# Differential attention with TensorE's order written out piece by piece

## The chip, the cores and the metric

One core of one Trainium2 chip. The metric is the device time of one execution in microseconds (us). Times inside the execution are microseconds from the start of the profiled span.

## The reference

A trunk of four layers over 256 tokens of width 1024, in float32. Each layer is a feed-forward half step, a token mixer and a second feed-forward half step, with a norm before and after each. The mixers of the four layers are sparse attention (layer 0), stick-breaking attention (layer 1), differential attention (layer 2) and sparse attention again (layer 3). Only the third is touched by the change:

```python
qa, ka, va = jnp.split(h @ w_in, 3, axis=-1)
q = qa.reshape(B, T, DIFF_HEADS, 2, DIFF_DH)      # 8 heads, 2 maps each, 64 wide
k = ka.reshape(B, T, DIFF_HEADS, 2, DIFF_DH)
v = va.reshape(B, T, DIFF_HEADS, 2 * DIFF_DH)
...
    s = jnp.einsum('bqhmd,bkhmd->bhmqk', qb, k).astype(f32) * scale
    s = jnp.where(dist >= 0, s - slopes[None, :, None, None, None] * dist, NEG)
    p = jax.nn.softmax(s, axis=-1)
    a = p[:, :, 0] - lam_full * p[:, :, 1]
    o = jnp.einsum('bhqk,bkhe->bqhe', a.astype(v.dtype), v)
    o = rms_norm(o, subln_g) * (1.0 - lam_init)
...
return sweep_blocks(block, T) @ w_out
```

So each head makes two softmax maps, subtracts one from the other, multiplies by the values and norms the result; an output projection follows.

## The kernel before

The whole trunk is one program. Activations stay on the chip; the weights stream through it once. A weight piece of 512 KB is loaded into one of seven raw buffers by the queue of SyncE (SP), then split into a high part (a cast on ScalarE, line 135) and a low part (a subtraction on VectorE, line 136). High and low parts have nine buffers each (`NSPLIT`). Every projection is three products per row block: high by high, and the two mixed ones. For the sums the activations too are held as a high and a low part, `yh` and `yl`.

PSUM has eight banks in three pools: four named `acc` (projections, value products, output sums), two `mm` (scores) and two `tp` (transposes).

The tokens stand in two halves of 128, `h` = 0 and 1; causality lets half 0 see 128 keys and half 1 see 256. In the differential mixer the eight heads stand in two groups of four. The four combinations of group and half are named a (group 0, half 0), b (group 0, half 1), c (group 1, half 0) and d (group 1, half 1), and each is worked in two units of two heads. One unit has these steps: scores (line 663, into both `mm` banks), the softmax of `softmax_alibi` (VectorE reads the banks, adds the distances and takes the maximum at line 666; ScalarE exponentiates at line 674; ScalarE and VectorE scale and subtract at lines 1137 and 1138), transposes of the result (line 1145), their copy to SBUF, and the value products (line 1150). When a combination's two units are through, its four heads are normed (lines 1158 to 1165), transposed (line 1170) and written to `yh` and `yl` (`put_o`, lines 627 and 628) for the output projection (lines 405 to 409).

A scheduler turns the program's text into an order for each engine. The text is the first guess, and an instruction may move ahead of another on its engine where nothing forbids it. `tc.issue_after(ins)` forbids it: what is traced under it stays behind `ins` on the engine of `ins`. The helper `pin` (line 304) uses this to chain pieces of TensorE's work, so that each piece's matmuls stay behind the last matmul of the piece before; matmuls for the conditioning weights (`ada`) are left out of the chain. The sparse mixers (`Nsa`) already run a `plan` of pinned pieces and a `rest` of pinned output projections behind it. The differential mixer, like the stick-breaking one, is not pinned: its `plan` lists whole projections (192 matmuls of 256 columns for queries or keys of a part, less where pairs are named) and lets generators a to d advance by stages between them.

The mixer's end goes over into the next sublayer. `post` for half 0 (residual and norm of the output sums) and `pre` for half 0 (the next sublayer's norm, the transposes `p_y` of line 339, and the modulation) are traced between the mixer's body and its `tail`; the tail holds the output projections of half 1 that are left. `pre` is pinned only where the mixer is sparse:

```python
post(i, s, 0, cur.accs[0], last)
...
(pin if s == 1 and not i % 3 else lambda f: f())(lambda: gate.extend(pre(*subs[n + 1], 0)))
cur.tail()
```

Of the kernel before, what the change touches and what calls it, by code (L numbers as in the profile page):

```python
# [40 lines left out]
def trunk_kernel(ctx, tc, x, c, ada_w, ada_b, norm_g, ffn_w1, ffn_w2, nsa_w_in, nsa_cmp_pe, nsa_cmp_w1,  # L41
# [650 lines left out]
    class Nsa(Mixer):  # L692
# [11 lines left out]

        def run(self, plan):


            for op in plan.replace("\n", " ").split(";"):
                op, *args = op.split()
                if args and args[0] in "abcd":  # L710
                    pin(getattr(self.at[args[0]], op), *map(int, args[1:]))
                else:
                    pin(getattr(self, op), *map(int, args))

        def body(self):
            pinned[:] = []
            self.at = {c: self.Attend(self, *half) for c, half in zip("abcd", HALVES)}
            self.run(self.plan)

        def tail(self):  # L720
            self.run(self.rest)
# [157 lines left out]

        def weight(self, k):  # L880
            gate_on[:] = self.copied
            self.wo[k] = self.out_weight(k)
            gate_on[:] = []

        def o(self, h, k, n=None):

            ns = (0, 1) if n is None else (n,)
            accs = self.accs.setdefault(h, [None, None])
            for m in ns:
                if accs[m] is None:  # L890
                    accs[m] = bank("acc", [128, 512], f"o{h}{m}")
            tok = slice(h * 128, (h + 1) * 128)
            mm_acc(accs, yh[:, k, tok], yl[:, k, tok], self.wo[k], k == 0, k == KC - 1, ns)
# [201 lines left out]
    class Diff(Dense):  # L1095
        w_in, w_out = diff_w_in, diff_w_out
        q_scale = staticmethod(lambda j: 0.125 / dslopes[j])
        plan = [("proj", 1, 0,), ("proj", 0, 0,), 'a', ("proj", 1, 1,), 'b', 'a', ("proj", 0, 1,), 'c', 'b', 'ab', 'c', 'd', ("out_proj", 0, 0,), 'c', 'd', ("out_proj", 1, 0,), 'd']
# [24 lines left out]
        def attend(self, hg, h, _):  # L1123
            tok = slice(h * 128, (h + 1) * 128)
            po = bank("acc", [128, 4, 128], "p_o")

            def heads(hp):
# [41 lines left out]
            for j in range(4):  # L1169
                nc.tensor.transpose(p[:, j, :], o[:, j, :], ident)  # L1170
# [118 lines left out]
```

## Time and profile before

| | |
|---|---|
| median of 3 runs | 2169.16 us (2161.97 to 2175.18) |
| the profiled execution's own time | 2169.74 us |
| its span | 2167.9 us |
| TensorE busy in the span | 2096.4 us (97%) |
| VectorE, ScalarE busy | 1622.9 us (75%), 1119.8 us (52%) |
| mean granted clock of TensorE | 0.99 |
| differential mixer, from the last value projection to the next sublayer's first product | 1321.2 to 1420.4 us |

The span is the stretch from the first to the last instruction that the profile records. "Granted clock" is the share of the full clock that TensorE was given: 1.00 is 2.4 GHz, 0.50 is 1.2 GHz. The ends of matmuls are modelled, so neighbouring matmuls overlap in the rows; the distance between their starts is the pace.

### The profile page before, as it was taken

Reading aid. Unit: us, or ns where it says so; the run is one execution under the profiler, and the core shown is the slowest. Engines: PE = TensorE matmul, PEld = TensorE weight load, DVE = VectorE, ACT = ScalarE, POOL = GpSimd, SP = SyncE. Lnnn points to the kernel's source line nnn. Section 1 sums busy time; section 2 is a strip of 40 time slices with the busy share of each in tenths; the row PEclk is TensorE's granted clock in tenths of the full one; section 3 lists DMA queues with packets and bytes.
Section 4 is the critical chain, followed back from the end, with each engine's and each line's share of the span. In section 5 each row is a group of like instructions: output and inputs, shape, how many; then the busy total and the mean of one; then the engine's idle time right before and its main releaser. Section 6 shows DMA issues by size and latency. Waiting matters only on the chain.

```text
span 2167.9 us, 37376 instructions
## 1 busy us (share of the span) xinstructions
PE 2096.4 (97%) x14395; PEld 1856.1 (86%) x14395; DVE 1622.9 (75%) x2736; ACT 1119.8 (52%) x1989; POOL 67.3 (3%) x154
## 2 busy tenths in 40 slices
PE   5999999999999999999999999999999999999998
PEld 5999775899899979799989888789999997668998
DVE  7987866777798777677688858687779868767654
ACT  3444655644544456754464455664455445656443
POOL 1000000000000000100000000000000000000000
PEclk9999998999999999999999999999999999999999
DMA  9998752687699856388779958278869986545761
GB/s 316 335 348 287 252 137 78 215 287 262 199 330 312 282 186 222 122 278 277 256 235 330 313 170 297 78 240 274 275 203 330 308 276 194 163 118 172 241 200 59
DMA packets 338179, 512.55 MB, mean 236 GB/s; under 512 B 20832, under 2 KB 211256, under 8 KB 338000
## 3 DMA queue, kind: packets, MB, share of 16 engines
q1 hardware_dynamic: 329456, 501.15, 69.9%
q10 hardware_dynamic: 8544, 9.01, 1.4%
q8 instruction: 113, 1.85, 0.3%
q14 instruction: 66, 0.54, 0.1%
HBM read 507.91 MB, written 1.05 MB: 235 GB/s over the span
## 4 chain that ended last, share of the span: by engine, by line
PE 74%; DVE 11%; issue 5%; DMA 5%; ACT 4%; POOL 2%; ACTq 0%; SPq 0%; DVEq 0%; POOLq 0%
PE p_gu L386 12%; PE p_gu L388 12%; PE p_gu L387 12%; PE f L405 6%; PE f L406 6%; PE f L409 6%; DVE lo_w L136 3%; DMA raw_ada<-in_ada_w_dram 3%; PE p_o L909 1%; PE p_pr L386 1%; PE p_pr L387 1%; PE p_pr L388 1%; PE p_t L956 1%; POOL rx L325 1%; PE o L405 1%
## 5 line engine op out<-in xcount | busy, mean ns | idle before, releaser
L135 ACT CAST hi_w<-raw_w 128x1024 fp32r<-128x1024 f32 x528 | 551.5, 1055 | 325.6 <-PE f L409 113.4
L136 DVE TENSOR_TENSOR lo_w<-raw_w,hi_w 128x1024 fp32r<-128x1024 f32 x528 | 633.1, 1221 | 103.6 <-ACT hi_w L135 97.2
L386 PE MATMUL p_gu<-yh,hi_w 128*128 128x256 f32 x2368 | 665.6, 281 | 4.0 <-DVE yh L351 4.0
L387 PE MATMUL p_gu<-yl,hi_w 128*128 128x256 f32 x2368 | 660.9, 279 | 0.3 <-DVE yl L352 0.3
L388 PE MATMUL p_gu<-yh,lo_w 128*128 128x256 f32 x2368 | 661.0, 279 | 0.0
L386 PEld LDWEIGHTS p_gu<-yh,hi_w 128*128 128x128 f32 x2368 | 445.7, 188 | 17.3 <-DVE lo_w L136 6.2
L192 DVE SCALAR_TENSOR_TENSOR ada_acc<-raw_ada,cT,ada_acc 128x512 f32<-128x512 f32 x500 | 374.0, 749 | 103.3 <-DMA raw_ada<-in_ada_w_dram 95.3
L387 PEld LDWEIGHTS p_gu<-yl,hi_w 128*128 128x128 f32 x2368 | 446.0, 188 | 5.4 <-issue 1.7
L388 PEld LDWEIGHTS p_gu<-yh,lo_w 128*128 128x128 f32 x2368 | 445.8, 188 | 0.2
L405 PE MATMUL f<-hi_w,hb 128*128 128x512 f32 x704 | 275.8, 393 | 1.9 <-ACT hb L550 1.8
L406 PE MATMUL f<-lo_w,hb 128*128 128x512 f32 x704 | 275.9, 392 | 0.0
L409 PE MATMUL f<-hi_w,hb 128*128 128x512 f32 x704 | 228.3, 391 | 0.0
L550 ACT CAST hb<-sg 128x256 fp32r<-128x256 f32 x148 | 60.2, 407 | 199.6 <-DVE sg L549 198.1
L548 ACT ACTIVATE sg<-p_gu 128x256 f32<-128x256 f32 x148 | 56.3, 380 | 204.1 <-PE p_gu L388 183.8
L405 PEld LDWEIGHTS f<-hi_w,hb 128*128 128x128 f32 x704 | 132.3, 188 | 29.2 <-ACT hb L550 4.7
L409 PEld LDWEIGHTS f<-hi_w,hb 128*128 128x128 f32 x704 | 131.6, 188 | 29.3 <-DVE hb L551 1.9
L406 PEld LDWEIGHTS f<-lo_w,hb 128*128 128x128 f32 x704 | 132.2, 188 | 24.5 <-DVE lo_w L136 0.3
L549 DVE TENSOR_TENSOR sg<-sg,p_gu 128x256 f32<-128x256 f32 x148 | 61.5, 416 | 79.0 <-ACT sg L548 78.8
L551 DVE TENSOR_TENSOR hb<-sg,hb 128x256 fp32r<-128x256 f32 x148 | 62.4, 422 | 35.2 <-ACT hb L550 35.2
L350 ACT ACTIVATE y<-p_y,ab 128x128 f32<-128x128 f32 x184 | 67.2, 465 | 29.7 <-PE p_y L339 24.2
L387 PE MATMUL p_pr<-yl,hi_qk 128*128 128x256 f32 x256 | 71.8, 281 | 0.0
L386 PE MATMUL p_pr<-yh,hi_qk 128*128 128x256 f32 x256 | 71.5, 281 | 0.0
(273 smaller groups left out, 3191.6 us busy)
## 6 DMA issues: line engine op xcount, KB each, us to landing
raw_w<-in_ffn_w_dram SPq DMA_DIRECT2D x528, 512.0 KB
raw_ada<-in_ada_w_dram SPq DMA_DIRECT2D x288, 512.0 KB
raw_kv<-in_nsa_w_in_dram SPq DMA_DIRECT2D x16, 512.0 KB
raw_q<-in_nsa_w_in_dram SPq DMA_DIRECT2D x16, 512.0 KB
raw_cw<-in_nsa_cmp_w_dram SPq DMA_DIRECT2D x16, 512.0 KB
raw_wo<-in_nsa_w_out_dram SPq DMA_DIRECT2D x32, 256.0 KB
raw_qk<-in_sb_w_in_dram SPq DMA_DIRECT2D x16, 512.0 KB
raw_qk<-in_diff_w_in_dram SPq DMA_DIRECT2D x16, 512.0 KB
```

The costliest lines, as they stand in the source:

```text
L135: nc.scalar.copy(hi, src)
L136: nc.vector.tensor_sub(lo, src, hi)
L192: nc.vector.scalar_tensor_tensor(a, r[:, j], cT[:, k:k + 1], a, op0=OP.mult, op1=OP.add)
L350: nc.scalar.activation(y[:, j, :], p[:, j, :], AF.Identity, scale=ab[:, k:k + 1], bias=ab[:, 8 + k:9 + k])
L386: nc.tensor.matmul(o, cols(wh), yh[:, k, :], start=first and k == 0, stop=False)
L387: nc.tensor.matmul(o, cols(wh), yl[:, k, :], start=False, stop=False)
L388: nc.tensor.matmul(o, cols(wl), yh[:, k, :], start=False, stop=last and k == KC - 1)
L405: nc.tensor.matmul(acc[n], lh, wh[:, sl], start=first, stop=False)
L406: nc.tensor.matmul(acc[n], lh, wl[:, sl], start=False, stop=False)
L409: nc.tensor.matmul(acc[n], ll, wh[:, sl], start=False, stop=last)
L549: nc.vector.tensor_mul(sg, sg, p[:, 1, :])
L551: nc.vector.tensor_sub(hl[:, cc, :], sg, hh[:, cc, :])
```

## The change

The differential mixer becomes a pinned one. `run`, `body`, `tail`, `weight` and `o` move from `Nsa` to a new class `Pinned`, which `Nsa` and `Diff` inherit, and nothing changes in `Nsa` itself. In `Diff` the generators give way to a written plan whose pieces are:

- `pj which part j [rows]`: keys (1) or queries (0) of two heads, 48 matmuls, or with `rows` one half of the row blocks, 24 matmuls;
- `S x n`, `T x n`, `P x n`: scores with softmax, transposes with their copy (always on ScalarE), and value products of unit n of combination x; `P x 1` also norms x;
- `N x`: transposes of the normed heads and `put_o`;
- `weight k`: load and split of output weight k, issued behind the latest copy of a `T`;
- `o h k [n]`: output products of half h with weight k, six matmuls, or three for one column half n.

`pre` of half 0 is pinned behind any pinned mixer, so now behind `Diff` too, and the pieces of `rest` are pinned behind it.

```diff
+    class Pinned(Mixer):
+        def run(self, plan):
+            for op in plan.replace("\n", " ").split(";"):
+                op, *args = op.split()
+                if args and args[0] in "abcd":
+                    pin(getattr(self.at[args[0]], op), *map(int, args[1:]))
+                else:
+                    pin(getattr(self, op), *map(int, args))
+        def body(self):
+            pinned[:] = []
+            self.at = {c: self.Attend(self, *half) for c, half in zip("abcd", HALVES)}
+            self.run(self.plan)
+        def tail(self):
+            self.run(self.rest)
+        def weight(self, k):
+            gate_on[:] = self.copied
+            self.wo[k] = self.out_weight(k)
+            gate_on[:] = []
+        def o(self, h, k, n=None):
+            ns = (0, 1) if n is None else (n,)
+            accs = self.accs.setdefault(h, [None, None])
+            for m in ns:
+                if accs[m] is None:
+                    accs[m] = bank("acc", [128, 512], f"o{h}{m}")
+            tok = slice(h * 128, (h + 1) * 128)
+            mm_acc(accs, yh[:, k, tok], yl[:, k, tok], self.wo[k], k == 0, k == KC - 1, ns)
...
-    class Nsa(Mixer):
+    class Nsa(Pinned):
...
-    class Diff(Dense):
+    class Diff(Pinned, Dense):
...
-        plan = [("proj", 1, 0,), ("proj", 0, 0,), 'a', ("proj", 1, 1,), 'b', 'a', ("proj", 0, 1,), 'c', 'b', 'ab', 'c', 'd', ("out_proj", 0, 0,), 'c', 'd', ("out_proj", 1, 0,), 'd']
+        plan = """pj 1 0 0; pj 0 0 0; S a 0; pj 1 0 1 0; S b 0; pj 1 0 1 1; pj 0 0 1; S a 1; T a 0; pj 1 1 0 0; P a 0; T b 0; S b 1;
+                  pj 1 1 0 1; P b 0; T a 1; pj 0 1 0 0; P a 1; pj 0 1 0 1; S c 0; T b 1; pj 1 1 1 0; P b 1; S d 0; pj 1 1 1 1;
+                  T c 0; pj 0 1 1 0; P c 0; weight 0; pj 0 1 1 1; N a; S c 1; T d 0; weight 1; N b; S d 1; P d 0; weight 2; o 0 0;
+                  weight 3; T c 1; o 0 1; weight 4; P c 1; T d 1; weight 5; o 0 2; weight 6; P d 1; o 0 3; weight 7; N c;
+                  o 1 0 0; o 1 1 0; o 0 4; o 0 5; N d; o 0 6; o 0 7; o 1 2 0; o 1 3 0"""
+        rest = """o 1 0 1; o 1 1 1; o 1 2 1; o 1 3 1; o 1 4 0; o 1 5 0; o 1 6 0; o 1 7 0; o 1 4 1; o 1 5 1; o 1 6 1; o 1 7 1"""
...
+        def pj(self, which, part, j, rows=None):
+            o, sc = ((self.qT, self.q_scale), (self.kT, None))[which]
+            if (which, part) not in self.w:
+                self.w[which, part] = self.columns(which, part, "qk")
+            ks = range(KC) if rows is None else range(KC // 2 * rows, KC // 2 * (rows + 1))
+            if ks[0] == 0:
+                self.pp = bank("acc", [128, 2, T], "p_pr")
+            p = self.pp
+            for q in range(2):
+                for k in ks:
+                    wh, wl = self.w[which, part][k]
+                    c = chunk(2 * j + q)
+                    nc.tensor.matmul(p[:, q, :], c(wh), yh[:, k, :], start=k == 0 and q == 0, stop=False, skip_group_check=True)
+                    nc.tensor.matmul(p[:, q, :], c(wh), yl[:, k, :], start=False, stop=False, skip_group_check=True)
+                    nc.tensor.matmul(p[:, q, :], c(wl), yh[:, k, :], start=False, stop=k == KC - 1, skip_group_check=True)
+            if ks[-1] == KC - 1:
+                j0 = 4 * part + 2 * j
+                if sc is None:
+                    evac(j, o[:, j0:j0 + 2, :], p)
+                else:
+                    nc.scalar.activation(o[:, j0, :], p[:, 0, :], AF.Copy, scale=sc(j0))
+                    nc.vector.tensor_scalar(o[:, j0 + 1, :], p[:, 1, :], sc(j0 + 1), None, op0=OP.mult)
+        class Attend:
+            def S(self, hp):
...
+                r = softmax_alibi(h, qk, [sc[:, 2 * m:2 * m + 2] for m in range(2)],
...
+            def T(self, hp):
+                h, sc = self.h, self.sc[hp]
+                p = bank("tp", [128, 2, h + 1, 128], "p_t")
+                for e in range(2):
+                    for kb in range(h + 1):
+                        nc.tensor.transpose(p[:, e, kb, :], sc[:, e, kb * 128:(kb + 1) * 128], ident)
+                t = self.t[hp] = s2([128, 2, h + 1, 128], "aT")
+                self.diff.copied = [nc.scalar.copy(t, p).ins]
+            def P(self, hp):
+                h = self.h
+                if self.po is None:
+                    self.po = bank("acc", [128, 4, 128], "p_o")
+                for e in range(2):
+                    hd = 4 * self.hg + 2 * hp + e
+                    for kb in range(h + 1):
+                        nc.tensor.matmul(self.po[:, 2 * hp + e, :], self.t[hp][:, e, kb, :],
+                                         self.diff.v[:, kb, hd * 128:(hd + 1) * 128], start=kb == 0, stop=kb == h)
+                if not hp:
+                    return
...
+            def N(self):
+                p = bank("tp", [128, 4, 128], "p_ot")
+                for j in range(4):
+                    nc.tensor.transpose(p[:, j, :], self.o[:, j, :], ident)
+                put_o(p, 4 * self.hg, self.h)
...
-            (pin if s == 1 and not i % 3 else lambda f: f())(lambda: gate.extend(pre(*subs[n + 1], 0)))
+            (pin if isinstance(cur, Pinned) else lambda f: f())(lambda: gate.extend(pre(*subs[n + 1], 0)))
```

## Rows read from the trace of the kernel before

**Rows 1.** The page's busy times: us, share of the span, instructions.

```profile
PE 2096.4 (97%) x14395; PEld 1856.1 (86%) x14395; DVE 1622.9 (75%) x2736; ACT 1119.8 (52%) x1989; POOL 67.3 (3%) x154
```

**Rows 2.** Busy by stretch: length, engines, granted clock, DMA share, GB/s.

```profile
1321.20:1420.40 99.20, 93.61 (x643) 82.05 (x643) 70.88 (x187) 62.79 (x170) 5.16 (x6) 0.97 0.49 167
...
1321.20:1343.50 22.30, 22.30 (x191) 22.13 (x190) 16.86 (x20) 10.81 (x13) 0.00 (x0) 1.00 1.02 378
...
1390.90:1407.30 16.40, 15.56 (x82) 12.76 (x81) 7.51 (x26) 9.37 (x39) 2.01 (x2) 0.98 0.00 1
```

**Rows 3.** TensorE's timeline in the mixer: start, length, operation, idle before.

```profile
1343.51 0.72 PE L663 MATMUL p_s<-qkv 64*128 64x128 f32 x8
1344.15 1.98 PE L281 MATMUL p_gate<-ada_acc,ones 128*128 128x512 f32 x4
...
1346.94 0.28 PE L387 MATMUL p_pr<-yl,hi_qk 128*128 128x256 f32 x1
...
1357.91 0.28 PE L388 MATMUL p_pr<-yh,lo_qk 128*128 128x256 f32 x1
1358.12 1.13 PE L663 MATMUL p_s<-qkv 64*128 64x256 f32 x8
1359.18 0.66 PE L1145 MATMUL p_t<-ident,sc 128*128 128x128 f32 x4
...
1378.84 1.95 PE L1150 MATMUL p_o<-qkv,aT 128*128 128x128 f32 x16
1380.63 0.38 PE L1170 MATMUL p_ot<-ident,o_n 128*128 128x128 f32 x2
...
1414.14 1.06 PE L339 MATMUL p_y<-ident,xn 128*128 128x128 f32 x8 [0.41 <-DVE xn L355]
1414.96 0.48 PE L406 MATMUL o<-lo_wo,yh 128*128 128x512 f32 x1
...
1420.17 0.40 PE L409 MATMUL o<-hi_wo,yl 128*128 128x512 f32 x1
```

**Rows 4.** TensorE's waits in 1321.2 to 1420.4: us, times, longest.

```profile
PE p_s L663 <- DVE sm_m L666: 4.3, 3, 2.4
```

**Rows 5.** Busy by microsecond where the clock falls and returns.

```profile
1384.00:1385.00 1.00, 0.56 (x2) 0.53 (x3) 1.00 (x7) 0.97 (x7) 0.00 (x0) 0.90 0.82 266
...
1391.00:1392.00 1.00, 1.00 (x5) 0.83 (x4) 1.00 (x5) 0.80 (x4) 0.00 (x0) 0.68 0.00 0
...
1924.00:1925.00 1.00, 1.00 (x4) 0.19 (x2) 0.96 (x4) 0.09 (x1) 0.00 (x0) 0.56 0.05 16
...
1934.00:1935.00 1.00, 1.00 (x5) 0.81 (x4) 0.00 (x0) 1.00 (x2) 0.00 (x0) 0.82 0.00 0
```

**Rows 6.** Timelines of ScalarE and VectorE at the first query weights.

```profile
1327.72 1.05 ACT L135 CAST hi_qk<-raw_qk 128x1024 fp32r<-128x1024 f32 x1 [2.65 <-DMA raw_qk<-in_diff_w_in_dram]
...
1328.95 1.22 DVE L136 TENSOR_TENSOR lo_qk<-raw_qk,hi_qk 128x1024 fp32r<-128x1024 f32 x1
```

**Rows 7.** Timelines in layer 0's mixer, scores directly behind their projection.

```profile
260.31 0.47 ACT L775 ACTIVATE qkv<-p_pr,qscale 128x256 f32<-128x256 f32 x1
...
260.84 0.48 DVE L776 TENSOR_SCALAR qkv<-p_pr,qscale 128x256 f32<-128x256 f32 x1
...
260.84 1.36 PE L927 MATMUL p_s<-qkv 64*128 64x256 f32 x8 [1.72 <-ACT qkv L775]
```

**Rows 8.** Timelines of TensorE and VectorE, scores and softmax of c 1.

```profile
1377.60 0.70 PE L663 MATMUL p_s<-qkv 64*128 64x128 f32 x4 [0.49 <-DVE sm_m L666]
...
1384.83 0.64 DVE L1138 SCALAR_TENSOR_TENSOR sc<-sc,sm_r 128x128 f32<-128x128 f32 x2
```

**Rows 9.** TensorE's timeline, the last output products of token half 0.

```profile
1406.84 0.63 PE L409 MATMUL o<-hi_wo,yl 128*128 128x512 f32 x2
```

**Rows 10.** TensorE's timeline, two more of its idle stretches.

```profile
1361.33 1.82 PE L663 MATMUL p_s<-qkv 64*128 64x256 f32 x8 [1.49 <-DVE sm_m L666]
...
1923.29 1.58 PE L909 MATMUL p_o<-pT,vc 15*64 15x512 f32 x4 [2.52 <-DVE pT L631]
```

More of the change, by code (lines that the diff above doesn't have):

```diff
@@ L703, in trunk_kernel @@
         rest = """o 1 0 1; o 1 1 1; o 1 2 1; o 1 3 1; o 1 4 0; o 1 5 0; o 1 6 0; o 1 7 0; o 1 4 1; o 1 5 1; o 1 6 1; o 1 7 1"""
[L705 to L721, printed above, removed]
         def head(self, h, gate):
@@ L1139, in heads @@
                                                    sc[:, e, :], op0=OP.mult, op1=OP.add)
-                def second():
-                    p = bank("tp", [128, 2, h + 1, 128], "p_t")
-                    for e in range(2):
-                        for kb in range(h + 1):
-                            nc.tensor.transpose(p[:, e, kb, :], sc[:, e, kb * 128:(kb + 1) * 128], ident)
-                    t = s2([128, 2, h + 1, 128], "aT")
-                    evac(hp, t, p)
-                    for e in range(2):
-                        for kb in range(h + 1):
-                            nc.tensor.matmul(po[:, 2 * hp + e, :], t[:, e, kb, :],
-                                             self.v[:, kb, hds[e] * 128:(hds[e] + 1) * 128], start=kb == 0, stop=kb == h)
@@ L1152, in heads @@
-                return second
-            stages = self.pipeline([lambda hp=hp: heads(hp) for hp in range(2)])
-            next(stages)
-            yield
-            next(stages)
-            o = s2([128, 4, 128], "o_n")
-            ss = small([128, 4], "ssd")
-            for j in range(4):
-                nc.scalar.activation(junk[:, :128], po[:, j, :], AF.Square, accum_out=ss[:, j:j + 1])
-            nc.vector.tensor_scalar(ss, ss, 1.0 / 128, EPS, op0=OP.mult, op1=OP.add)
-            nc.gpsimd.tensor_tensor(ss, ss, mhalf, op=OP.pow)
@@ new lines, in P @@
+            def P(self, hp):
[9 more added lines that the diff above has]
+                    return
+                po = self.po
+                o = self.o = s2([128, 4, 128], "o_n")
+                ss = small([128, 4], "ssd")
+                for j in range(4):
+                    nc.scalar.activation(junk[:, :128], po[:, j, :], AF.Square, accum_out=ss[:, j:j + 1])
+                nc.vector.tensor_scalar(ss, ss, 1.0 / 128, EPS, op0=OP.mult, op1=OP.add)
+                nc.gpsimd.tensor_tensor(ss, ss, mhalf, op=OP.pow)
+                for j in range(4):
+                    nc.vector.scalar_tensor_tensor(o[:, j, :], po[:, j, :], ss[:, j:j + 1], self.diff.sg, op0=OP.mult, op1=OP.mult)
```

34 lines of the change are left out of this document (8 added, 26 removed).

## The prediction

> **What bounds the kernel now.** The page's busy shares come first: TensorE is busy for 97% of the span, VectorE for 75%, ScalarE for 52% [rows 1]. So time is gained only where TensorE idles, runs at its lower clock, or runs at less than its stream rate, and the change touches one stage: the mixer of layer 2, from the last value projection (1321.2) to the first product of the next feed-forward block (1420.4). The table by stretch gives this stage 99.2 us, 93.6 of them with TensorE busy [rows 2]. All else is taken to shift as a whole: a TensorE-bound kernel passes on what this stage loses or gains.
>
> A busy row overstates useful work, so I count the work by the spacing of matmul starts in TensorE's timeline [rows 3].
> - Query and key projections: the matmuls from 1346.94 to 1357.91 are 95, so 94 gaps of 0.1167 us. The stage has 382: 44.6 us.
> - Output projection: from 1414.96 to 1420.17 there are 22 gaps of 0.237 us. The stage has 96: 22.7 us.
> - Scores, eight instructions for each unit: of the first token half 0.64 us (1343.51 to 1344.15), of the second 1.06 (1358.12 to 1359.18), four units of each: 6.8 us.
> - Value products: 16 in 1.79 (1378.84 to 1380.63), so 48 take 5.4 us.
> - Transposes: eight in 0.82 (1414.14 to 1414.96), so 24 + 16 + 8 take 4.9 us. The gate's row sums: 2.0 us.
>
> Together 86.4 us. The stage therefore loses 99.2 - 86.4 = 12.8 us. Of that the list of waits puts 4.3 us on score matmuls that wait for VectorE to read the previous scores out of the two score banks [rows 4]. 3.4 us are clock: TensorE's granted clock is 0.50 between about 1384.8 and 1391.6 [rows 5], the level of 1.2 GHz, 6.85 us at half rate. The other 5.1 us are small waits and changes of shape between instruction streams. 12.8 us is all that the change could win, 0.6% of 2169.
>
> **The change part by part.** The instructions stay the same in number and shape; the evacuation of the transposed scores moves wholly to ScalarE, which has room. What changes is TensorE's order, which becomes fixed piece by piece. I walk through the new order and ask at each piece what it waits for.
>
> *The waits for score banks go.* Scores stand one unit at a time between half projections of 24 matmuls (24 x 0.1167 = 2.8 us), in which VectorE reads the banks. 4.3 us gone, except that two units of the last quarter (c 1 and d 1) have only eight transposes between them (0.8 us) against four reads and their start on VectorE of about 1.4: 0.6 us stays.
>
> *Query weights come earlier than they can.* Before, both halves of the first key projection (96 matmuls, 11.2 us) stand ahead of the queries. Now one half does, so the queries start at about 1326.8, and their last quarter of rows (k 6 and 7) is due at 1326.8 + 18 x 0.1167 = 1328.9. Its high part was cast only when its load landed at 1327.72, and its low part is ready at 1328.95 + 1.22 = 1330.2 [rows 6]. The DMA engines are full there (share 1.02) [rows 2], so it can't come sooner: 1.3 us lost, bounds 0 and 2.5 (a second split late).
>
> *A projection directly ahead of the scores that need it.* S a 0, S a 1 and S c 0 follow the query piece that they read; S c 1 has one set of transposes between. This occurs in the first layer's mixer, whose order is already pinned: ScalarE scales one chunk at 260.31 (0.47), VectorE the other at 260.84 (0.48), and TensorE had idled 1.72 us [rows 7], a part of it because ScalarE had come late from a cast. Without that, two such evacuations one behind the other make 1.0 us; three of these, and 0.4 for the fourth, 3.4 us, bounds 1.5 and 5.5. The wait stops the next half projection, whose weights are ready.
> The Trainium skill (PSUM — Partial Sum Buffer, section "PSUM bank collisions raise a hardware error") says that two engines must not touch one bank at once, so the two scalings of one projection bank follow each other. By it the price is 1.0 us each, with both side by side about 0.6 (one scaling and a handoff), and the sum 1.3 us less; the rows agree with the first, 260.84 being after the end of the scaling that began at 260.31.
>
> *Transposes of the last scores.* Between S c 1 and T c 1 TensorE has 0.4 + 0.4 + 1.1 + 0.9 + 1.4 = 4.2 us of its own work. Before, the same unit took from 1377.60 to 1384.83 + 0.64 = 1385.5 until its scores were ready, 7.9 us less 0.6 of scores [rows 8], while VectorE also split weights; now seven of the eight output weights are to be split in this very stretch, since they are issued behind the copies of T c 0 and later ones. With the 0.6 us of the score banks, that leaves 7.3 - 4.2 - 0.6 = 2.5 us of wait if the chain stays as slow, and none if VectorE serves it first. I take 1.7, nearer to the row, and 1.5 for T d 1, whose rows are twice as long but which has a product more ahead of it: 3.2 us, bounds 0 and 7. Queued behind them are output projections that could have run.
>
> *The next layer's transposes are pinned too.* This is the largest term. Residual, norm and scaling of token half 0 start when its last output product ends. Before, that matmul starts at 1407.07 (the second of the pair from 1406.84) [rows 9], and the transposes p_y start at 1414.14 [rows 3]: 7.1 us, of which TensorE idled only 0.4, because 25 matmuls of token half 1 and four transposes ran meanwhile. Now only o 1 2 0 and o 1 3 0, six matmuls or 1.4 us, stand between o 0 7 and the pinned p_y, and the remaining 36 output matmuls (8.5 us) are pinned behind it. With the chain at 6.7 (0.4 less, as VectorE then has no other output to split) the wait is 6.7 - 0.23 - 1.4 = 5.0 us, bounds 4.5 and 6. Nobody can fill it: all that is left on TensorE is behind it in its queue. In turn the next block's input is ready long before its first product, which no longer matters.
>
> *The clock after that wait.* TensorE's clock fell to 0.50 in this stage after the longest wait for score banks, 2.4 us [rows 4, 5], and in the last layer's mixer after an idle of 2.52, there from about 1924.1 to 1934.4 [rows 5, 10]. An idle of 1.49 us at 1361 brought no fall [rows 10]. A wait of 5.0 us is longer than any of these. I price it as the fall that goes: 6.85 us at half rate, 3.4 us; bounds 0 and 5.1 (10.3 us at half). The old fall goes, since its wait goes.
> The Trainium skill (TensorE: Matmul & The Clock Gate, section "What's actually happening") has 1.2 GHz as the state that an idle TensorE returns to and that activity lifts. By it this term is 3.4, without it 0; the trace agrees with it at both falls.
>
> *More changes of shape.* Going from a projection to scores costs 0.09 (from 1357.91 + 0.12 to 1358.12) [rows 3]; I take 0.2 us for the way there and back. The new order has some 17 rounds, the old 11: 1.2 us more. Of the old 5.1 about 1.9 are small waits counted anew above, so this remainder is 5.1 - 1.9 + 1.2 = 4.4, bounds 3 and 5.5.
>
> *The load queue.* On SP's queue the loads of the next block's weights stand behind those of the output weights, which now leave the raw buffers later, since their splits wait for the copies of T c 0, T d 0 and those after. That costs nothing: the DMA engines moved nothing from 1391 to 1407 [rows 2], and the first product comes later than before.
>
> **Sum.** New losses 0.6 + 1.3 + 3.4 + 3.2 + 5.0 + 3.4 + 4.4 = 21.3 us against 12.8: 8.5 us more. The profiled execution took 2169.74, 0.6 above the median of 2169.16, so 2178.2 for it and about 2177.6 beside the median: 0.4% slower, inside the 0.5% (10.8 us) that a measurement of this kernel can tell from no change.
>
> **The rivals.**
> - *As summed* (chance 0.5): 2177.6, own range 2172 to 2182.
> - *A second clock fall* (0.22). The waits before T c 1 and T d 1, 3.2 us within some 6, bring the clock down as the 2.4 us of before did. It decides once one of the two passes about 2.4 us. Price 3.4 and the longer wait itself, 1 to 4: 2182 to 2185, slower beyond the 0.5%. For it: VectorE's weight splits now fall there. Against: output products lie between the two.
> - *No clock fall at p_y* (0.18): by the clock's rows the unlikely side. 2177.6 - 3.4 = 2174, and with the waits before T c 1 and T d 1 halved 2172.5.
> - *The mixing wins* (0.1): weight splits stay out of the softmax chains' way, T c 1 and T d 1 don't wait, the gate's row sums fill two of the evacuation waits, and the clock holds. Place: the last quarter; it decides if the chain from S c 1 falls from 7.3 to 4.8 us, TensorE's own work there. Then 8.5 - 3.2 - 2 - 3.4 - 1.3 = -1.4 with the query weights in time: 2168. Faster than 0.5% would need 10.8 of 12.8 us back with p_y's 5.0 still lost: hardly possible, 0.03.
> - *The change does nothing of what it says* is not open: TensorE's order is in the program.
>
> **How the numbers follow.** The predicted time is that of the sum. All lower bounds together make 9.6 us of losses, 3.2 faster than before; all upper ones 32.2, 19.4 slower: 2166 to 2188.5. The range leaves out a little at the top and adds some of the runs' own spread (2161.97 to 2175.18) below: 2165 to 2187. Slower by over 0.5% (above 2180): 0.22 and a tenth of the rest, 0.29. Faster 0.03. Within: 0.68.
>
> **What would show it.** Right: an idle of 4.5 to 6 us on TensorE ahead of p_y of that mixer, with a granted clock of 0.50 behind it; no wait of scores on VectorE's reads above 1 us; p_gx some 8 us later after the last value projection. Wrong: p_y without a wait, its matmuls set among the output products; a wait before T d 1 of more than 4 us; a stage shorter than 99 us; or a changed time in the other layers.

## The result and the profile after

The changed kernel takes 2183.21 us (median of 11 runs, 2179.96 to 2191.17), the kernel before beside it 2172.32 (11 runs): ratio 1.0056, 95% interval 1.0043 to 1.0070, so 12.2 us slower (9.3 to 15.2); the two medians differ by 10.9. The forecast was 8.5 us more, 2177.6. The profiled execution took 2191.17 us, the longest of the 11. Behind the stage of the change it took 7.0 us more than the profile of before, 5.4 of them in the last layer's mixer, where the matmuls have the same order and the clock was lower. The windows view shows it from its key and value projection into the next block's first products, before and after (length, engines, granted clock, DMA share, GB/s):

```profile
1813.90:1981.50 167.60, 158.00 (x1002) 117.49 (x1001) 123.94 (x379) 99.23 (x261) 4.44 (x5) 0.97 0.54 159
1830.00:2003.00 173.00, 163.92 (x1001) 121.46 (x1000) 124.26 (x379) 99.15 (x262) 4.43 (x5) 0.93 0.52 154
```

So the whole spans are not compared here, only the stage of the change.

Page, busy times:

```profile
PE 2104.0 (96%) x14395; PEld 1859.7 (85%) x14395; DVE 1623.1 (74%) x2732; ACT 1121.1 (51%) x1993; POOL 66.0 (3%) x154
```

The work is that of [rows 1]. The stage from the last value projection to the next block's first product, by the same view, and under it the windows in which the clock falls:

```profile
1323.03:1434.90 111.87, 96.78 (x644) 83.62 (x643) 71.95 (x183) 65.03 (x175) 5.16 (x6) 0.94 0.43 145
1352.00:1354.00 2.00, 1.90 (x8) 1.06 (x9) 2.00 (x10) 0.37 (x1) 0.00 (x0) 0.81 0.90 246
1354.00:1356.00 2.00, 2.00 (x5) 0.90 (x4) 0.78 (x4) 0.89 (x5) 0.00 (x0) 0.50 0.88 313
1356.00:1358.00 2.00, 2.00 (x16) 2.00 (x16) 1.66 (x5) 1.45 (x6) 0.00 (x0) 0.84 0.29 115
1404.00:1406.00 2.00, 2.00 (x9) 1.72 (x8) 1.30 (x5) 2.00 (x3) 0.66 (x1) 0.61 0.71 234
1406.00:1408.00 2.00, 2.00 (x9) 1.81 (x9) 2.00 (x2) 0.90 (x4) 0.00 (x0) 0.54 0.06 23
1422.00:1424.00 2.00, 0.67 (x4) 0.70 (x5) 0.88 (x2) 0.00 (x0) 0.56 (x1) 0.50 0.00 0
1424.00:1426.00 2.00, 2.00 (x9) 1.81 (x9) 0.01 (x1) 1.55 (x5) 0.00 (x0) 0.50 0.00 0
1426.00:1428.00 2.00, 2.00 (x6) 1.58 (x5) 1.62 (x4) 2.00 (x5) 0.00 (x0) 0.50 0.00 0
1428.00:1430.00 2.00, 2.00 (x9) 1.64 (x8) 2.00 (x3) 2.00 (x3) 0.00 (x0) 0.92 0.00 0
```

The stage is 111.9 us against 99.2 [rows 2]: 12.7 more, as near to the 12.2 of the times as one execution of each kernel can tell. There are three clock falls where there was one [rows 5]. Each costs the missing share of its windows: 0.4 + 1.0 + 0.3 = 1.7 us, 0.8 + 0.9 = 1.7, and for the third, counted from 1423.33 where TensorE works again, 0.3 + 2.0 + 0.2 = 2.5.

TensorE's waits in the stage (us, times, longest):

```profile
PE p_y L339 <- DVE xn L355: 4.8, 1, 4.8
PE p_t L1182 <- DVE sc L1174: 3.1, 2, 2.0
PE p_o L1193 <- ACT aT L1184: 2.6, 2, 1.5
PE p_s L699 <- ACT qkv L1152: 2.0, 3, 1.1
PE p_s L699 <- DVE qkv L1153: 1.7, 2, 1.0
PE p_pr L1146 <- DVE lo_qk L136: 0.8, 1, 0.8
```

The score-bank waits of [rows 4] are gone; 15.0 us of others stand in their place. TensorE's timeline shows where (start, length, operation, idle before):

```profile
1350.60 0.49 PE L699 MATMUL p_s<-qkv 64*128 64x128 f32 x4 [1.09 <-ACT qkv L1152]
1352.10 0.49 PE L699 MATMUL p_s<-qkv 64*128 64x128 f32 x4 [1.01 <-DVE qkv L1153]
...
1386.34 0.71 PE L1193 MATMUL p_o<-qkv,aT 128*128 128x128 f32 x4 [1.54 <-ACT aT L1184]
...
1397.25 0.51 PE L1182 MATMUL p_t<-ident,sc 128*128 128x128 f32 x2 [1.11 <-DVE sc L1174]
...
1400.22 0.71 PE L1193 MATMUL p_o<-qkv,aT 128*128 128x128 f32 x4 [1.06 <-ACT aT L1184]
...
1402.91 0.74 PE L1182 MATMUL p_t<-ident,sc 128*128 128x128 f32 x4 [1.98 <-DVE sc L1174]
...
1423.33 1.94 PE L339 MATMUL p_y<-ident,xn 128*128 128x128 f32 x8 [4.79 <-DVE xn L355]
```

Every kind of wait but one is in the prediction's sum. The exception is P c 0 and P c 1, value products that wait for the copy of their transposed scores. ScalarE's timeline shows why for P c 0:

```profile
1384.66 0.56 ACT L667 COPY qkv<-p_pr 128x512 f32<-128x512 f32 x1
1385.12 0.91 ACT L1173 ACTIVATE sc<-sc,sm_r 128x256 f32<-128x256 f32 x2
1385.93 0.35 ACT L1184 COPY aT<-p_t 128x256 f32<-128x256 f32 x1
```

The transposes had been started at 1381.61. Their copy takes 0.35 us but stands behind the four exponentials of unit d 0 (from 1382.67), a key copy and a scaling, and starts 4.3 us later. The copy for P c 1 stands in the same way behind the exponentials of d 1: the last of them starts at 1399.32, the copy at 1399.82.

### The profile page after: what moved, and what is told of

Read it like the earlier page. It is cut to its first block, busy times and chain, and to the rows that moved or that the text cites. A ratio compares the mean times of both kernels' runs of the same rounds, so it can differ in the third digit from the quotient of the medians.

```text
span 2189.4 us, 37377 instructions
## 1 busy us (share of the span) xinstructions
PE 2104.0 (96%) x14395; PEld 1859.7 (85%) x14395; DVE 1623.1 (74%) x2732; ACT 1121.1 (51%) x1993; POOL 66.0 (3%) x154
## 3 DMA queue, kind: packets, MB, share of 16 engines
HBM read 507.91 MB, written 1.05 MB: 232 GB/s over the span
## 4 chain that ended last, share of the span: by engine, by line
PE 65%; DVE 13%; DMA 8%; issue 6%; ACT 5%; POOL 2%; DVEq 0%; SPq 0%; POOLq 0%; ACTq 0%
PE p_gu L386 10%; PE p_gu L387 10%; PE p_gu L388 10%; DMA raw_ada<-in_ada_w_dram 6%; PE f L405 6%; PE f L406 5%; PE f L409 5%; DVE lo_w L136 4%; DVE ada_acc L192 2%; PE p_o L912 2%; PE o L405 1%; PE p_t L959 1%; POOL rx L325 1%; DMA raw_w<-in_ffn_w_dram 1%; PE o L406 1%
## 5 line engine op out<-in xcount | busy, mean ns | idle before, releaser
L350 ACT ACTIVATE y<-p_y,ab 128x128 f32<-128x128 f32 x184 | 67.2, 466 | 32.6 <-PE p_y L339 27.9
L945 ACT ACTIVATE sc<-sc,sm_m 128x256 f32<-128x256 f32 (+1 forms) x128 | 56.6, 444 | 31.8 <-DVE sm_m L939 31.7
L446 PE MATMUL p_gx<-hi_w,yh 128*128 128x256 f32 x224 | 63.8, 285 | 0.0
```

The source lines that it names most:

```text
L350: nc.scalar.activation(y[:, j, :], p[:, j, :], AF.Identity, scale=ab[:, k:k + 1], bias=ab[:, 8 + k:9 + k])
L446: nc.tensor.matmul(p[:, 0], yh[:, k, tok], wg[k][0], start=st, stop=False)
```

## The experiments

Theory A: each wait is a stall of its own, it stops ready work behind it because the order is fixed, and the prices add, clock falls included. The rivals name another cause for each run. The expectations of the first four runs put the changed kernel's stage at 110.2 us, with an end at 1433.3; the first product starts at 1434.9, so 111.9 is the right number and differences are taken from it. Stages are of one profiled execution each; ratios are of all runs against the kernel before, timed in between.

| run | stage, us | ratio to before [95%] |
|---|---|---|
| before | 99.2 | 1 |
| changed kernel | 111.9 | 1.0056 [1.0043, 1.0070] |
| p_y not pinned | 105.7 | 1.0020 [1.0006, 1.0034] |
| more cover ahead of p_y | 105.8 | 1.0014 [1.0000, 1.0028] |
| copies on two engines | 107.9 | 1.0033 [1.0020, 1.0046] |
| filler ahead of p_y | 109.6 | 1.0027 [1.0016, 1.0039] |
| scores later | 107.2 | 1.0024 [1.0011, 1.0038] |
| nothing pinned | 98.2 | 0.9995 [0.9980, 1.0010] |
| last quarter | 110.8 | 1.0032 [1.0016, 1.0048] |
| cover, copies, scores | 98.7 | 0.9984 [0.9968, 1.0000] |
| and a late quarter | 99.5 | 0.9989 [0.9977, 1.0002] |
| and keys first | 97.9 | 0.9987 [0.9972, 1.0002] |
| late quarter, nothing pinned | 97.4 | 0.9990 [0.9974, 1.0006] |
| keys first, norm behind | 102.4 | 1.0000 [0.9986, 1.0015] |

A stage says where time went in one execution, not what a version takes on average. In all twelve experiments the times put the version lower against before than the stages do, by 0.1 to 4.6 us, and the part behind the stage, which has TensorE's matmuls in the same order but for some of the first two hundred or so, takes 745.5 to 754.5 us in the fourteen profiles.

**p_y not pinned.**

```diff
-            (pin if isinstance(cur, Pinned) else lambda f: f())(lambda: gate.extend(pre(*subs[n + 1], 0)))
+            (pin if isinstance(cur, Nsa) else lambda f: f())(lambda: gate.extend(pre(*subs[n + 1], 0)))
```

> The next sublayer's transposes p_y are no longer pinned; all else is as in the changed kernel. Theory A (the pinned p_y with only six matmuls of cover is the largest single loss: 4.8 us of wait and some 2.4 us of the clock that falls in it): the wait before p_y goes below 1 us, no clock of 0.50 follows it, and the stage from the last value projection to the next block's first product shrinks from 110.2 to 103 to 105 us; the whole kernel 5 to 7 us faster than the changed one, so still 3 to 6 slower than the kernel before. Theory B (the many small waits of the mixed pieces are the loss, and p_y's wait only collects slack, because the next block must wait for its input or its weights anyway): the first product p_gx waits instead, and the stage stays at 108 to 111 us.

**More cover ahead of p_y.**

```diff
-                  ... o 0 6; o 0 7; o 1 2 0; o 1 3 0"""
+                  ... o 0 6; o 0 7; o 1 2 0; o 1 3 0; o 1 4 0; o 1 5 0; o 1 6 0; o 1 7 0; o 1 0 1; o 1 1 1"""
```

> p_y stays pinned, but six more output pieces (18 matmuls, 4.2 us) stand ahead of it and six behind. Theory A: the wait before p_y is 0 to 1 us, the clock stays at 1.00 there, the stage takes 102 to 105 us, as in the run with p_y free. Theory B: the wait turns up at the first product of the next block, whose input needs some 6 us after p_y and now has only 5 us of matmuls over it; the stage stays above 108 us.

The line of p_y in the list of waits without the pin; with the cover it has 0.6:

```profile
PE p_y L339 <- DVE xn L355: 0.7, 1, 0.7
```

4.1 and 4.2 us of wait went, and with them the third clock fall; the other waits stayed as they were. The stage lost 6.2 and 6.1 us, which is 4.2 of wait and some 2 of clock. So the pin as such is harmless here: what counts is how many output products stand ahead of it.

**Copies on two engines.**

```diff
-                self.diff.copied = [nc.scalar.copy(t, p).ins]
+                self.diff.copied = [(nc.scalar.copy if hp % 2 else nc.vector.tensor_copy)(t, p).ins]
```

> The copy of the transposed scores goes back to VectorE for the first unit of each combination and stays on ScalarE for the second. Theory A: of the 2.6 us that value products wait for the copy on ScalarE, the 1.5 us at P c 0 go and the 1.1 us at P c 1 stay; the stage is 1 to 2 us shorter (108 to 109 us) and the kernel's time can't be told from the changed one. Theory B (ScalarE's queue, with casts and exponentials ahead of the copies, is what makes the last quarter slow): both waits and those before T c 1 and T d 1 shrink, the clock's fall around 1405 goes, 4 to 6 us in all.

Both waits of value products went (2.6 us); the transposes' line shows one wait where there were two:

```profile
PE p_t L1182 <- DVE sc L1174: 3.5, 1, 3.5
```

T c 1 no longer waits and T d 1 takes 1.5 us more: counted from S d 1, TensorE is through P c 1 2.2 us sooner, but the scores of d 1 are ready only 0.8 us sooner. The wait of P c 1 went although its copy stays on ScalarE, which theory A had not expected; rival B had it and T c 1 right, but not T d 1, and the clock's fall there stays. The stage is 4.0 us shorter: 1.8 ahead of S c 1, 1.5 from there to p_y, and 0.7 behind p_y. The last 0.7 are not the copies' doing: p_y waits as before, but the fall there is shorter (1.7 us lost instead of 2.5, by the windows). So the copies are worth some 3.3 us.

```profile
1420.18 1.69 PE L339 MATMUL p_y<-ident,xn 128*128 128x128 f32 x8 [4.80 <-DVE xn L355]
```

**Filler ahead of p_y.** Twenty matmuls whose sums nobody reads stand between o 1 3 0 and p_y.

```diff
+        def fill(self, n):
+            p = bank("acc", [128, 512], "p_fill")
+            for _ in range(n):
+                nc.tensor.matmul(p, yh[:, 0, 0:128], self.wo[0][0][:, 0:512], start=True, stop=True)
```

> Twenty matmuls of 512 columns (4.7 us) that nothing reads are pinned between o 1 3 0 and p_y; they do work that the reference does not ask for. They cover the wait without moving anything else, so this separates the clock's price from the wait's. Theory A: p_y starts when it did relative to the last output product of token half 0 (6.2 us after it), the clock stays at 1.00, and the stage is 2 to 3 us shorter (107 to 108.5 us). Rival (the clock falls for another reason, such as the thin work ahead of it, or its return costs nothing here because something else is waited for): the stage stays at 110 to 111 us.

```profile
1414.65 4.83 PE L1134 MATMUL p_fill<-hi_wo,yh 128*128 128x512 f32 x20
...
1419.62 1.06 PE L339 MATMUL p_y<-ident,xn 128*128 128x128 f32 x8
```

The wait is replaced by work of the same length, the clock stays at 1.00, and p_y's eight transposes take 1.06 us instead of 1.94. The stage is 2.3 us shorter: that is the price of the clock fall after p_y by itself, in agreement with the 2.5 read from the windows. The price is not fixed, though. The same wait of 4.8 us stands ahead of p_y in the changed kernel and in the runs with the copies on two engines, the scores later and the last quarter. From the start of p_y to the next block's first product these take 11.6, 10.9, 10.7 and 12.0 us, and 9.3 with the filler: the fall costs 1.4 to 2.7.

**Scores later.** Each `S` stands one half projection later than in the changed plan:

```diff
+        plan = """pj 1 0 0; pj 0 0 0; pj 1 0 1 0; S a 0; pj 1 0 1 1; S b 0; pj 0 0 1; T a 0; pj 1 1 0 0; S a 1; P a 0; T b 0;
+                  pj 1 1 0 1; S b 1; P b 0; pj 0 1 0 0; T a 1; pj 0 1 0 1; P a 1; pj 1 1 1 0; S c 0; T b 1; pj 1 1 1 1; P b 1; S d 0;
+                  pj 0 1 1 0; T c 0; weight 0; pj 0 1 1 1; P c 0; N a; S c 1; ...
```

> Only the order of pieces in the first three quarters differs from the changed kernel: each set of scores stands one half projection later, so that 24 projection matmuls (2.8 us) lie between a query piece and the scores that read it. Baselines for the stage from the last value projection to the first product of the next block: 99.2 us before, 111.9 us in the changed kernel. Theory A (waits are local and their prices add): the 3.7 us in which scores wait for the scaled queries go, and with them the first clock fall (some 1.7 us), since what went ahead of it was two such waits; stage 106 to 107, time about 5 us under the changed kernel; the other waits (p_y 4.8, transposes 3.1, products 2.6) stay. Rival B (the softmax chains set the pace): the scores' results come later by what the scores were moved, so transposes and value products wait for them instead; the sum of TensorE's waits stays within 1 us of the changed kernel's 15, stage above 110.

The stage is just above what theory A said, but only in part for its reason. The 3.7 us are gone at all three places, and 1.7 came anew at S c 1 (0.9 for ScalarE and 0.8 for VectorE), which did not wait in the changed kernel:

```profile
1383.18 0.49 PE L699 MATMUL p_s<-qkv 64*128 64x128 f32 x4 [0.88 <-ACT qkv L1152]
```

Its queries' projection ends near 1380.6, but by ScalarE's timeline their scaling starts at 1382.77, behind unit d 0's exponentials, a weight cast (1.04 us) and d 0's scaling (0.91), which now fall there. The query weights cost 0.8 more, the gate's row sums wait 0.6 for a copy, the copies cost the value products 0.9 less. In all the waits are 1.1 us less. Of the 4.7 us by which the stage is shorter, 4.1 lie ahead of the first output product, and the first clock fall (1.7) is gone there; 0.9 is the cheaper fall behind p_y, again not the edit's doing; 0.3 are lost between.

**Nothing pinned.** `run` calls the pieces without `pin`, and `pre` is not pinned; the text is that of the changed plan.

> The same pieces written in the same sequence as the changed kernel, but none of the mixer of layer 2 is pinned, nor the transposes of the next block's input: the scheduler may move single matmuls past each other again. Theory A (the fixed order is what costs, because a wait stops everything behind it): output products and projections fill the waits, p_y goes behind token half 1 products as before; waits in the stage together under 7 us, one clock fall at most, stage 100 to 104. Rival B (the sequence itself, scores behind their projection and late weights, costs, fixed or not): like the version with only p_y free, stage 105 to 107. Rival C: the scheduler, which goes by its own costs, spoils the new sequence: stage above 108.

```profile
PE p_ot L1216 <- DVE o_n L1211: 1.5, 1, 1.5
PE p_t L1188 <- DVE sc L1180: 1.5, 2, 1.2
PE p_o L1199 <- ACT aT L1190: 1.0, 1, 1.0
PE p_y L339 <- DVE xn L355: 0.7, 1, 0.7
PE p_s L699 <- DVE qkv L1159: 0.4, 1, 0.4
```

That is TensorE's list of waits. 15.0 us of waits become 5.1, three falls one, 111.9 us become 98.2. The timeline shows single matmuls passing each other, here the first of the two transposes of T c 1, taken between output products as it comes ready:

```profile
1391.37 0.30 PE L1188 MATMUL p_t<-ident,sc 128*128 128x128 f32 x1 [0.27 <-DVE sc L1180]
1391.42 0.48 PE L409 MATMUL o<-hi_wo,yl 128*128 128x512 f32 x1
```

The sequence of the plan, as a text for the scheduler, is thus as good as the old one; all of the loss, 13.7 us, came from fixing this sequence: 6.2 at p_y, 7.5 in the mixer, clock falls included.

**Last quarter.**

```diff
-                  weight 3; T c 1; o 0 1; weight 4; P c 1; T d 1; weight 5; o 0 2; weight 6; P d 1; o 0 3; weight 7; N c;
+                  weight 3; o 0 1; T c 1; o 0 2; weight 4; o 0 3; P c 1; weight 5; T d 1; weight 6; weight 7; P d 1; N c;
```

> Only the last quarter differs from the changed kernel: the output products o 0 1 and o 0 2 stand ahead of and behind T c 1, o 0 3 ahead of P c 1, and the splits of output weights 4 to 7 come one or two pieces later. Theory A: the waits before T c 1 (1.1), P c 1 (1.1) and T d 1 (2.0) fall from 4.2 together to at most 2.5, and the second clock fall (some 1.7 us) goes if no wait there passes 1.5; stage 108 to 110. The wait of P c 0 (1.5) and p_y's 4.8 stay. Rival B (the chain from S d 1 over its transposes, products and norm to N d sets the end of this quarter): the products taken forward are missing behind it, so N c or N d waits instead by as much, and the stage stays within 1 us of 111.9.

The waits of T c 1, P c 1 and T d 1 fell from 4.2 us to 1.2, but 1.0 came at P d 1 and 0.8 at a weight and at N d. The second fall stayed, though no wait of the quarter passes 1.3 us: theory A had it gone. From the first output product to p_y the quarter takes 27.9 us instead of 28.8, so it gained 0.9, less than theory A's 2 to 4, while rival B had nothing gained but what came back. The rest of the stage's 1.1 us lies outside the quarter: the query weights wait 1.0 longer, the fall behind p_y costs 0.4 more, and 1.6 less are spent between, because this execution does not have the first clock fall. The two waits at S a 1 are those of the changed kernel, with the same order around them, and yet the clock holds:

```profile
1346.03 0.49 PE L699 MATMUL p_s<-qkv 64*128 64x128 f32 x4 [1.09 <-ACT qkv L1152]
1347.53 0.49 PE L699 MATMUL p_s<-qkv 64*128 64x128 f32 x4 [1.01 <-DVE qkv L1153]
```

```profile
1340.00:1356.00 16.00, 13.90 (x107) 11.88 (x106) 12.04 (x34) 10.22 (x28) 0.00 (x0) 1.00 0.61 202
```

So the first fall is not certain with these waits: the profiles of the changed kernel and of the first four experiments, which share this order, all have it, and this one has not.

**Cover, copies and scores together.** The second, third and fifth edits in one kernel.

> Three edits together: scores one half projection later, six more output products of token half 1 ahead of the pinned p_y, and the copies of the transposed scores of the first unit on VectorE instead of ScalarE. Theory A (prices add): 111.9 less 6.1 for the cover, 4.0 for the copies and 5 for the scores makes 97 us, 2 us under the 99.2 of before; no wait above 2 us but one at the transposes of the last quarter, at most one clock fall; time within 0.3% of before, more likely under it than over. Rival B (waits move on to the next chain): the gains overlap, the last quarter's transposes wait for longer (above 5 us in sum), stage 101 to 104 and the time 0.1 to 0.3% above before.

```profile
PE p_t L1182 <- DVE sc L1174: 3.5, 1, 3.5
```

The stage fell by 13.2 of the 15.1 that the prices add up to. The missing 1.9 is mostly counted twice: the prices of the copies and of the scores hold 0.7 and 0.9 us of a cheaper fall behind p_y, and the cover takes that whole fall away; and the scores' price was taken as 5 where it had been 4.7. Without these the prices are 6.1, 3.3 and 3.8, together 13.2. So they add, as theory A had it. That they do so to a tenth is partly chance: at T d 1 the clock is at 0.50 for 6.8 us here, and was for 3.4 in the run with the copies. Against before the time is 0.16% less, at the edge of its interval: a tie, or a gain of at most a few us.

**A late quarter.** On top of that:

```diff
-                  weight 3; T c 1; o 0 1; weight 4; P c 1; T d 1; weight 5; o 0 2; weight 6; P d 1; o 0 3; weight 7; N c;
+                  weight 3; T c 1; o 0 1; weight 4; P c 1; o 0 2; weight 5; o 0 3; T d 1; weight 6; P d 1; weight 7; N c;
```

> The version with scores half a projection later, more cover ahead of p_y and copies shared between two engines (stage 98.7, 3.5 us of wait before T d 1 and a clock fall behind it), with one more edit: the output products o 0 2 and o 0 3 and the splits of their weights stand ahead of T d 1, P d 1 ahead of N c. Theory A (what is missing before T d 1 is TensorE work whose operands are ready): the weights 2 and 3 are split by 1389.4 and 1390.5 there, T d 1 was ready at 1392.1, so two products of 1.4 us from 1389.4 end where it is ready; the wait falls from 3.5 to under 1.5 us (of o 0 2 on its weight, P d 1 on its copy) and the clock holds; stage 94 to 96, time about 3 us under the version without the edit and 5 under before. Rival B (the chain behind T d 1 sets the end of the quarter): N c, N d or the products behind them wait as long as T d 1 did; stage 97.5 to 99.

A miss for theory A: both products went in as planned, and T d 1 waits 3.3 us all the same, since its scores are ready 3 us later. TensorE's line, then VectorE's and ScalarE's:

```profile
1394.99 0.74 PE L1182 MATMUL p_t<-ident,sc 128*128 128x128 f32 x4 [3.30 <-DVE sc L1174]
```

```profile
1388.48 3.48 DVE L136 TENSOR_TENSOR lo_wo<-raw_wo,hi_wo 128x1024 fp32r<-128x1024 f32 x3
...
1394.11 0.35 DVE L1205 SCALAR_TENSOR_TENSOR o_n<-p_o,ssd,subg 128x128 f32<-128x128 f32 x1 [1.12 <-POOL ssd L1203]
1394.37 0.87 DVE L1174 SCALAR_TENSOR_TENSOR sc<-sc,sm_r 128x256 f32<-128x256 f32 x2
```

```profile
1387.35 2.00 ACT L135 CAST hi_wo<-raw_wo 128x1024 fp32r<-128x1024 f32 x2
...
1391.23 0.26 ACT L1201 ACTIVATE junk<-p_o 128x128 bf16<-128x128 f32 x1
...
1392.68 0.89 ACT L1173 ACTIVATE sc<-sc,sm_r 128x256 f32<-128x256 f32 x2
```

Two queues make the 2.9 us by which d 1's scores come later than in the version before. On ScalarE two weight casts instead of one stand ahead of d 1's exponentials, which start 0.9 us later (1389.24, before 1388.31). The other 2 us are the norm of c's output, which stands ahead of d 1's scaling on both engines: four squares on ScalarE from 1391.23, where it was two, and on VectorE the wait for GpSimd.

**Keys first.** As the late quarter, with "pj 1 0 0; pj 1 0 1; pj 0 0 0; pj 0 0 1 0; S a 0; pj 0 0 1 1; S b 0; pj 1 1 0 0; S a 1; T a 0; pj 1 1 0 1; S b 1; P a 0; pj 0 1 0 0; T b 0; T a 1; pj 0 1 0 1; P b 0; P a 1; ..." as the start of the plan.

> As the version with the late quarter, and with both halves of the first key projection ahead of the query projection, as in the kernel before, so that the query weights are due 5.6 us later; scores, transposes and products of the first two quarters are set closer together for it. Theory A: the wait for the low part of the query weights (0.8 to 1.8 us in the runs so far) goes and nothing else changes; stage 1 to 1.5 us shorter than the version with the late quarter. Rival B: between S b 0 and T b 0, and S a 1 and T a 1, only some 7.5 us of TensorE work are left, and a chain of softmax takes 6 (first token half) to 10 us (second): T b 0 waits 1 to 3 us, stage 1 to 2 us longer.

The wait for query weights (1.5 us in the late quarter) is gone and no other came; the stage is 1.6 us shorter, as theory A had it. The times cannot be told apart.

**Late quarter, nothing pinned.**

> The pieces of the version with the late quarter in the same sequence, but none pinned: the scheduler may move single matmuls past each other, as in the unpinned version of the changed kernel (stage 98.2). Theory A (pinning costs only where a wait lies ahead of ready work): where the pinned sequence has hardly a wait left, freeing it gains or loses under 1.5 us against the pinned one. Rival B (pinning costs by itself, whatever the sequence): 3 us or more shorter than the pinned one. Rival C (the scheduler's own costs spoil a good sequence): 2 us or more longer.

97.4 us against 99.5 in the stage, 0.9990 against 0.9989 in the ratio. Theory A's bound is passed in the stage and rival B's not reached; the times show no difference. The test is not as clean as the theory asks: the pinned version still has 7.2 us of waits, the free one 5.1, so what pinning costs where nothing waits stays open.

**Norm behind.** Keys first, and P c 1 and the weights 4 and 5 moved behind T d 1.

```diff
-                  weight 3; T c 1; o 0 1; weight 4; P c 1; o 0 2; weight 5; o 0 3; T d 1; weight 6; P d 1; weight 7; N c;
+                  weight 3; T c 1; o 0 1; o 0 2; o 0 3; T d 1; weight 4; P c 1; weight 5; P d 1; weight 6; weight 7; N c;
```

> The version with the keys first (stage 97.9), with the second value product of c, P c 1, moved from ahead of o 0 2 to behind T d 1, and weight 4 behind T d 1 too. P c 1 brings with it the norm of c's output: four squares on ScalarE (1.5 us) and a wait of VectorE for GpSimd (1.1 us), which stood ahead of the scaling of d 1's scores. Theory A (the 3.3 us before T d 1 are those queues of ScalarE and VectorE): without them d 1's scores are ready some 2.5 us sooner, T d 1 waits under 1 us, the clock holds there; N c, whose norm now starts later, waits 1 to 2.5; stage 95 to 97, time 1 to 2 us less. Rival B (the whole chain of the last quarter, softmax and norm, has no room, in whatever order): N c or the output products behind it wait 3 us or more, with the clock fall there; stage 97.5 to 99, time unchanged.

T d 1 waits 0.9 us instead of 3.3, so theory A named the right queues; the norm and the two weights moved together, so their shares are not told apart. But N c waits 7.2, more than theory A said, and the stage is longer than either theory had it:

```profile
1400.03 1.16 PE L1210 MATMUL p_ot<-ident,o_n 128*128 128x128 f32 x4 [7.20 <-DVE o_n L1205]
```

```profile
1392.60 4.83 DVE L136 TENSOR_TENSOR lo_wo<-raw_wo,hi_wo 128x1024 fp32r<-128x1024 f32 x4 [2.09 <-ACT hi_wo L135]
```

The two weights that I had moved back, and the two behind them, are now all cast and split in the middle of c's norm: on ScalarE a cast of 1.05 us stands ahead of each of c's four squares, and on VectorE the splits take 4.8 us. What left one chain's way fell into the next one's.

## Why the prediction was right in kind and short in size

The direction, the place and the size within the range were right: slower, in this stage alone, 2183.2 inside 2165 to 2187. By 12.2 us it lies just outside the half per cent, a case that had 0.29, and outside the 2172 to 2182 of the sum's own case. The forecast started from 2169.16, while the kernel before had 2172.32 in these runs, so the differences, 8.5 and 12.2, are what compares. Of the signs, the wait ahead of p_y (4.8) with a clock of 0.50 behind it came, and no score waits for VectorE's reads; the next block's first product comes 12.7 later, not 8. A changed time in the other layers was to be a sign of being wrong; the 7.0 us behind the stage are mostly the clock in the last mixer, with the same order, and other versions took as little as 745.5 us there. The stage lost 111.9 - 86.4 = 25.5 us where the sum had 21.3:

| term | forecast | measured |
|---|---|---|
| score banks | 0.6 | 0 |
| query weights late | 1.3 | 0.8 |
| scores behind their projection | 3.4 | 3.7 |
| T c 1 and T d 1 | 3.2 | 3.1 |
| p_y | 5.0 | 4.8 |
| copies on ScalarE | 0 | 2.6 |
| clock | 3.4 | 5.9 |
| shape changes, the rest | 4.4 | 4.6 |

The last row is what is left over, not measured by itself. The terms built from rows of a neighbouring order held within 0.6 us as sums. Two terms did not, the copies and the clock, and two of the sums that held did so partly by luck.

- *"The evacuation of the transposed scores moves wholly to ScalarE, which has room."* ScalarE is busy for half the span, but in order: the copy stood behind the exponentials of the next unit. The copies shared between two engines took both of these waits away. A mean busy share says nothing of the queue at one moment.
- *Scores behind their projection.* The sum had 1.0 us at each of S a 0, S a 1 and S c 0 and 0.4 at S c 1; measured are 0.5, 2.1, 1.2 and nothing. It had left out that an engine may come late from other work. At S a 1 both did: a weight cast stands ahead of ScalarE's scaling, and a weight split ahead of VectorE's, first ScalarE's row, then VectorE's:

```profile
1349.23 1.03 ACT L135 CAST hi_qk<-raw_qk 128x1024 fp32r<-128x1024 f32 x1
```

```profile
1350.49 1.22 DVE L136 TENSOR_TENSOR lo_qk<-raw_qk,hi_qk 128x1024 fp32r<-128x1024 f32 x1
1351.62 0.42 DVE L1153 TENSOR_SCALAR qkv<-p_pr 128x256 f32<-128x256 f32 x1
```

- *T c 1 and T d 1.* They had 1.7 and 1.5 and waited 1.1 and 2.0. The forecast put seven weight splits into the stretch between S c 1 and T c 1; one stands there on VectorE, and two from 1397.37, when T c 1 had started.
- *The clock.* The fall after p_y was forecast at 3.4 and cost 2.5 by the windows, 2.3 by the filler, and 1.4 to 2.7 in other runs with the same wait. The rival of a second fall came true beside it, 1.7 us, though not from its stated point: no wait there came near 2.4; three of 1.1, 1.1 and 2.0 us stood ahead of it, at T c 1, P c 1 and T d 1. A third fall, 1.7 us, came behind S a 1 after two waits of 1.1 and 1.0, both shorter than the 1.49 that had brought no fall [rows 10]. The prediction priced falls by the longest single idle; here falls also came behind several short ones close together, though not in every execution. In the last-quarter version the second fall begins at 1398.3, inside a wait of 1.0 us at P d 1, with only 0.4 and 1.2 us of wait in the 7 us ahead of it. Whether the waits alone bring these falls, or the short pieces of work between them have a part in it, no run separates.

The Trainium skill (TensorE: Matmul & The Clock Gate, section "What's actually happening") has 1.2 GHz as the state that idleness returns to. The filler agrees: with TensorE at work in place of 4.8 us of idle the clock stayed at 1.00. On the scalings of a query bank the Trainium skill (PSUM — Partial Sum Buffer, section "PSUM bank collisions raise a hardware error") has two engines not touch one bank at once, and the changed kernel agrees: ScalarE's scaling started at 1335.45 and took 0.38, VectorE's started at 1335.86.

What is not shown: why the first fall comes in one execution and not in another, and why one wait of 4.8 us costs 1.4 us of clock and another 2.7. That the last quarter has little room is argued from the orders tried, which wait 4.2 us there (changed kernel), 3.1 (last quarter), 3.5 (cover, copies and scores), 4.0 (late quarter) and 8.3 (norm behind); it is not a bound.

## What to carry to other kernels

A fixed order costs what its waits hold up: before pinning a piece, ask what ready work stands behind it and when its operand comes, and put that much ready work ahead of it. For an operand made by another engine, follow that engine's queue by its timeline at that moment, not its busy share, and expect work that is moved out of one chain to land in the next. Where prices of single edits are to be added, ask whether two of them hold the same gain. Several short waits close together can cost the clock as one long one does, so count them together.

## What the runs showed of the hardware

Two executions with the same order and the same waits of 1.09 and 1.01 us differ in the granted clock, 0.50 in one and 1.00 in the other, while the work behind them was the same four row sums (3.19 us in the changed kernel, 1.88 in the last-quarter version). I had expected the clock to follow from the order; what else it follows stays open. In the late-quarter version the granted clock was still 1.00 over the 4 us that hold the 3.3 us of idle, and fell only when TensorE was working again (with one more wait of 0.7 us between, at P d 1):

```profile
1391.00:1395.00 4.00, 0.70 (x4) 0.25 (x3) 2.35 (x7) 2.48 (x12) 1.01 (x1) 1.00 0.88 280
1395.00:1401.00 6.00, 5.33 (x23) 4.53 (x24) 4.17 (x8) 4.78 (x11) 0.00 (x0) 0.72 0.50 162
```

In the keys-first version, with the same wait of 3.3 us at the same place, the clock had fallen inside the wait: 0.84 was granted over 1391 to 1392, and TensorE began again at 1392.45.
